# Scaling one token half only, and a second gate-up group with four seven-product pairs

## The chip, the cores and the metric

The kernel runs on one core of a Trainium2 chip. Time is device microseconds from launch to end; three runs of the kernel before gave 1823.62, 1824.14 and 1824.19 us, so the median is 1824.14 us. The engines are named as in the profile: PE is TensorE (matrix products), PEld its weight loads, DVE is VectorE, ACT is ScalarE, POOL is GpSimd and SP is SyncE, which here only issues DMAs.

## The reference

One encoder layer on 256 tokens of width 2048, in float32:

```python
ff = swiglu(rms_norm(x, pre_norm_ffn1), w_ffn1_gate_up, w_ffn1_down)   # 2048 -> 2 x 5632 -> 2048
x = x + 0.5 * rms_norm(ff, post_norm_ffn1)
h = rms_norm(x, pre_norm_mix)            # then HGRN2 heads and window attention on h @ w_mix_in
x = x + rms_norm(mixed, post_norm_mix)   # mixed = concat(y_h, y_a) @ w_mix_out
ff = swiglu(rms_norm(x, pre_norm_ffn2), w_ffn2_gate_up, w_ffn2_down)
x = x + 0.5 * rms_norm(ff, post_norm_ffn2)
```

`swiglu` is `silu(x @ gate) * (x @ up)` and then the down projection. The change is in the gate-up part of both feed-forward layers.

## The kernel before

**Exact products.** Every float32 operand is split into two parts, `h` (rounded) and `l` (the rest); a product is three matmuls, h by h, h by l and l by h. ScalarE writes `h` (line 176), VectorE subtracts to get `l` (line 177).

**Tiling of gate-up.** The 5632 gate and 5632 up columns are taken in 11 groups of 512 + 512 columns. Within a group the 2048 rows are taken in 8 pairs of two 128-row tiles. One pair of one group is one weight tile `raw` of 1 MB: four blocks of 128 x 512, b11 and b12 (gate and up of the first row tile), b21 and b22 (of the second). The tokens make a 2 x 2 block as well: two row tiles by two token halves of 128 tokens. A pair is thus a 2 x 2 by 2 x 2 block product. A plain pair takes 8 block products, that is 24 matmuls. A seven-product pair takes 7 (`products`, a Strassen-Winograd scheme), that is 21 matmuls, and needs sums of weight blocks and of token blocks. The four weight sums are made by an accumulating DMA that GpSimd issues (line 953, the up columns added onto b11 and b12 after b11 has been split) and two VectorE additions (lines 967 and 968); they also mean that the pair is split in three halves of 128 x 1024 and one first block of 128 x 512 instead of two halves. The token sums are made once for each pair by `sums_in` (lines 1069, 396, 399, 400 and one split), and serve all later groups.

**Which pairs.** `MIXED_IN = (2, 4, 5, 6)` lists the seven-product pairs. The first group is all plain. The second group (g = 1) has pairs 2 and 4 as sevens, every later group has all four. In the second group of the kernel before, the token sums of pairs 5 and 6 are made inside it (after pairs 4 and 5) for the third group.

**The scale of the norm.** The row norm gives one factor for each token, `rs2` (a column of two: token half 0 and 1). It is known only when the first group is under way. The first group therefore runs on unscaled tokens and applies `rs2` when it leaves PSUM (`units`, lines 1092 and 1097). For the token sums of a seven the two halves must have comparable scale, so the power of two of each factor (`two`) is spread over partitions (`spread`, a product with a matrix of ones, line 279) and multiplied into the token tiles in place (`even`, line 1062); the later groups apply what is left (`rest`).

**Order of the work.** From the second group on, each of TensorE, VectorE and ScalarE runs the order in which the code is written (`manual_schedule`). In the first group a scheduler places the instructions. Weight tiles come in through five buffers; `plan` sorts the loads by the time at which a pair is wanted, a seven-product pair some pairs ahead (`PREPARED`), and `prepare` splits its first block and issues the accumulating DMA. At the end of a group `boundary` adds the seven-product parts to the plain parts with eight VectorE additions (lines 1167 to 1177), between which TensorE does the last pair's products bank by bank.

Of the kernel before, what the change touches and what calls it, by code (L numbers as in the profile page):

```python
# [37 lines left out]
def hymba_layer_kernel(  # L38
# [25 lines left out]
    nc = tc.nc  # L64
# [18 lines left out]
    def pb():  # L83
        return psum.tile([P, 512], F32, tag="pb", name=nm("pb"))
# [16 lines left out]
    ones = const.tile([P, P], F32, tag="ones", name="ones")  # L101
# [35 lines left out]
    R = const.tile([P, T], F32, tag="R", name="R")  # L137
    scales = const.tile([P, 8], F32, tag="scales", name="scales")
    rs2, two, rest = (scales[:, 2 * i : 2 * i + 2] for i in range(3))

    def load(src, between=None, pool=rawp, **kw):
        raw = pool.tile([P, 2048], F32, tag="raw", name=nm("raw"), **kw)
# [122 lines left out]
    def power_and_rest():  # L265

        for part, a, b in ((two, 0x7F800000, 0), (rest, 0x007FFFFF, 0x3F800000)):
            nc.vector.tensor_scalar(
                part.bitcast(I32), rs2.bitcast(I32), a, b, ALU.bitwise_and, ALU.bitwise_or
            )  # L270

    def spread(factor=rs2):

        ps = pb()
        for m in range(2):
            nc.vector.tensor_scalar(
                R[:, m * P : (m + 1) * P], ident, factor[:, m : m + 1], None, ALU.mult
            )
        nc.tensor.matmul(ps[:, :T], ones, R, start=True, stop=True)
        nc.vector.tensor_copy(R, ps[:, :T])  # L280


    def xcol(xt, k, part=None):
# [599 lines left out]
    NG = DFF // 512  # L883
# [3 lines left out]
    MIXED_IN = (2, 4, 5, 6)  # L887
# [8 lines left out]
    class Gated(Blocks):  # L896
# [19 lines left out]

        def plan(self):

            self.here = {g: MIXED_IN if g > 1 else MIXED_IN[:2] for g in range(1, NG)}
            wanted = []  # L920
            for g in range(1, NG):
                for u in range(KT // 2):
                    before = PREPARED[u] if u in self.here[g] else u
                    wanted.append((g * KT // 2 + before, g, u))
            self.wanted = [at[1:] for at in sorted(wanted)]
            self.raws, self.firsts, self.split_of = {}, {}, {}
            self.lasting = []
# [96 lines left out]
    def ffn(gated, w_dn, post_gain, again, gain=None, lead=None, aside=None):  # L1024

        with ExitStack() as st:
# [31 lines left out]

            def even(u):

                x = gated.tiles[u].rearrange("p k i t -> p (k i) t")
                nc.vector.tensor_tensor(
                    x, x.bitcast(F32), R[:, None, :].to_broadcast([P, 4, T]), ALU.mult
                )

            def sums_in(u):
                x = gated.tiles[u].bitcast(F32)
                whole = room_for("z").rearrange("p (k t) -> p k t", k=2)
                nc.vector.tensor_tensor(whole, x[:, :, 0, :], x[:, :, 1, :], ALU.add)
                ws = sums_of(whole, room_for("s").rearrange("p (j t) -> p j t", j=4))  # L1070
                apart = u == MIXED_IN[1]
                w = (gated.room if apart else work).tile(
                    [P, 4, 2, P], F32R, tag="sp", name=nm("xs"), bufs=1 if apart else 3
                )
                split_act(w[:, :, 0, :], w[:, :, 1, :], ws)
                gated.sums[u] = w
# [63 lines left out]
            nc.scalar.activation(warm[:, 0:2], rs2, AF.Silu)  # L1140
            last = KT // 2 - 1
            for u in range(gated.pos, KT // 2):
                gated.work(u + 1)
                if u == 4:
                    power_and_rest()
                    spread(two)
                for done in {4: (0, 1, 2), 5: (3, 4), 6: (5, 6), 7: (7,)}.get(u, ()):
                    even(done)
                    if done in MIXED_IN[:2]:
                        sums_in(done)  # L1150
                if u == 5 and aside:
                    aside()
            gated.plan()
# [46 lines left out]
            def pair_ahead(g, u):  # L1200

                ahead = gated.splits(g, u + 1)
                next(ahead)
                if u + 1 == MIXED_IN[1]:
                    gated.prepare(g, MIXED_IN[3])
                next(ahead)
                for one in gated.take(g, u):
                    one()
                for _ in ahead:
                    pass  # L1210
                if g == 1 and u in (4, 5):
                    sums_in(MIXED_IN[u - 2])
                if u == 5 and 1 < g <= AWAY // 2 + 1:
                    put_away(2 * g - 4)
                    put_away(2 * g - 3)
# [163 lines left out]
    gated = Gated(w_ffn1_gate_up[0], two_banks())  # L1379
# [134 lines left out]
    with ExitStack() as s2:  # L1514
# [389 lines left out]
        g = gates(1)  # L1904
# [13 lines left out]
        gated = Gated(w_ffn2_gate_up[0], two_banks())  # L1918
# [80 lines left out]
```

## Time and profile before

| | us |
|---|---|
| median of three runs | 1824.14 |
| the profiled execution, its own time | 1824.91 |
| its span, first to last instruction | 1822.8 |
| PE busy | 1808.7 |
| DVE busy | 1607.0 |
| ACT busy | 1133.8 |
| POOL busy | 160.4 |

The times of the profile's views are counted from the span's start. A row of the timeline gives start, length, engine, source line, operation, tile written and tiles read, and in brackets the idle time ahead of it with what ended it. Lengths of neighbouring instructions of one engine overlap, since the next starts before the last one's write is through; where a cost is wanted, the step from one start to the next is used. In the first feed-forward layer the first group ends near 58 us and the second near 102 us; in the second layer the same work lies near 1168 and 1212 us.

### The profile page before, as it was taken

What the parts mean: (1) busy time and instruction counts of PE and PEld (TensorE: products, weight loads), DVE (VectorE), ACT (ScalarE), POOL (GpSimd) and SP (SyncE); (2) the same over time, 40 slices, a digit from 0 to 9 for tenths busy, and PEclk for the clock granted to TensorE, in tenths of its full rate; (3) what the DMA queues carried; (4) which work ended last, traced back from release to release, by engine and by line L of the source; (5) the groups of instructions that cost most, each with busy time, mean ns of one, the idle gap of its engine ahead of it and who ended that gap; (6) DMA issues with size and microseconds to landing.
All of it is one profiled execution on the core that took longest, in us unless ns stands there. A gap on an engine that the chain in (4) does not pass through costs nothing.

```text
span 1822.8 us, 23456 instructions
## 1 busy us (share of the span) xinstructions
PE 1808.7 (99%) x8426; PEld 1502.4 (82%) x8426; DVE 1607.0 (88%) x2059; ACT 1133.8 (62%) x1504; POOL 160.4 (9%) x153
## 2 busy tenths in 40 slices
PE   9999999999999999999999999999999999999998
PEld 6888888888888888888888888888888888888886
DVE  7999999999989989476787798999999999999987
ACT  7466666665665657476587556556666666566663
POOL 1011111111011100000000000001111111011110
PEclk9999999999999999999999999999999999999999
DMA  8789999998698995555554456789999998699894
GB/s 303 226 229 285 279 281 253 252 261 254 219 343 271 288 311 188 199 180 176 164 173 150 162 208 240 244 235 269 280 278 266 255 248 248 193 345 303 267 307 164
DMA packets 211508, 446.54 MB, mean 245 GB/s; under 512 B 11720, under 2 KB 46624, under 8 KB 210624
## 3 DMA queue, kind: packets, MB, share of 16 engines
q1 hardware_dynamic: 180032, 385.14, 60.4%
q0 software_dynamic: 31360, 59.91, 18.9%
q8 instruction: 66, 1.08, 0.2%
q14 instruction: 50, 0.41, 0.1%
HBM read 432.41 MB, written 12.60 MB: 244 GB/s over the span
## 4 chain that ended last, share of the span: by engine, by line
PE 95%; ACT 2%; DVE 2%; DMA 1%; issue 0%; SPq 0%; POOL 0%; DVEq 0%; ACTq 0%; POOLq 0%
PE pa L442 41%; PE pb L442 36%; PE pa L310 5%; PE pa L315 3%; PE pa L365 2%; PE pa L363 2%; PE pa L364 2%; DMA raw<-in_w_ffn_gate_up_dram 1%; DVE l L177 1%; PE pa L1117 1%; PE pb L1117 1%; PE pb L1720 0%; PE pb L1694 0%; PE pb L1798 0%; ACT h L176 0%
## 5 line engine op out<-in xcount | busy, mean ns | idle before, releaser
L176 ACT CAST h<-raw 128x1024 fp32r<-128x1024 f32 (+1 forms) x863 | 852.0, 1014 | 469.3 <-PE pb L442 151.0
L177 DVE TENSOR_TENSOR l<-raw,h 128x1024 fp32r<-128x1024 f32 (+1 forms) x863 | 984.5, 1171 | 133.8 <-ACT h L176 101.6
L442 PE MATMUL pa<-h,xt 128*128 128x512 f32 x1104 | 387.7, 392 | 0.1
L442 PE MATMUL pb<-h,xt 128*128 128x512 f32 x952 | 340.1, 392 | 0.4 <-DVE pb L1170 0.4
L442 PEld LDWEIGHTS pa<-h,xt 128*128 128x128 f32 x1104 | 207.2, 188 | 44.4 <-DVE xt L232 0.6
L442 PE MATMUL pa<-l,xt 128*128 128x512 f32 x552 | 215.4, 390 | 0.6 <-DVE l L177 0.5
L442 PEld LDWEIGHTS pb<-h,xt 128*128 128x128 f32 x952 | 178.6, 188 | 43.3 <-DVE pb L1177 3.7
L442 PE MATMUL pb<-l,xt 128*128 128x512 f32 x476 | 185.5, 390 | 0.0
L442 PE MATMUL pb<-h,ht 128*128 128x512 f32 x452 | 159.2, 389 | 0.0
L442 PE MATMUL pa<-h,ht 128*128 128x512 f32 x452 | 159.1, 389 | 0.0
L953 POOL DMA_DIRECT2D raw<-in_w_ffn_gate_up_dram x76 | 92.1, 1212 | 736.6 <-DVE l L177 639.1
L310 PE MATMUL pa<-xt,h 128*128 128x512 f32 x512 | 124.4, 392 | 0.2 <-ACT h L176 0.2
L442 PEld LDWEIGHTS pa<-l,xt 128*128 128x128 f32 x552 | 103.7, 188 | 21.4 <-DVE l L177 1.4
L310 PEld LDWEIGHTS pa<-xt,h 128*128 128x128 f32 x512 | 93.8, 188 | 18.6 <-ACT h L176 0.6
L442 PE MATMUL pa<-h,xs 128*128 128x512 f32 x304 | 108.8, 389 | 0.0
L442 PE MATMUL pb<-h,xs 128*128 128x512 f32 x304 | 105.9, 389 | 0.0
L442 PEld LDWEIGHTS pb<-l,xt 128*128 128x128 f32 x476 | 89.4, 188 | 17.0
L442 PEld LDWEIGHTS pb<-h,ht 128*128 128x128 f32 x452 | 84.8, 188 | 17.5
L442 PEld LDWEIGHTS pa<-h,ht 128*128 128x128 f32 x452 | 84.8, 188 | 17.5
L442 PE MATMUL pa<-l,ht 128*128 128x512 f32 x226 | 88.0, 389 | 0.0
L442 PE MATMUL pb<-l,ht 128*128 128x512 f32 x226 | 87.9, 389 | 0.0
L1255 POOL DMA_DIRECT2D raw<-in_w_ffn_down_dram x38 | 46.0, 1212 | 371.8 <-DVE la L177 317.6
(288 smaller groups left out, 2572.3 us busy)
## 6 DMA issues: line engine op xcount, KB each, us to landing
raw<-in_w_ffn_gate_up_dram SPq DMA_DIRECT2D x350, 512.0 KB, 6.0
raw<-in_w_ffn_down_dram SPq DMA_DIRECT2D x88, 1024.0 KB, 7.8
raw<-in_w_mix_in_dram SPq DMA_DIRECT2D x52, 1024.0 KB, 4.9
raw<-in_w_ffn_gate_up_dram POOLq DMA_DIRECT2D x76, 512.0 KB, 8.6
raw<-in_w_ffn_down_dram POOLq DMA_DIRECT2D x38, 512.0 KB, 10.0
raw<-in_w_mix_out_dram SPq DMA_DIRECT2D x16, 1024.0 KB, 5.2
ht<-away SPq DMA_DIRECT2D x24, 512.0 KB, 10.3
away<-ht SPq DMA_DIRECT2D x16, 512.0 KB, 7.3
```

Source lines behind the costliest of these rows:

```text
L176: nc.scalar.copy(hi, src)
L177: nc.vector.tensor_tensor(lo, src, hi.bitcast(F32), ALU.subtract)
L310: nc.tensor.matmul(slot[f], weights(hs, kk, f), xcol(xt, k), start=(k == 0), stop=(k == KT - 1))
L315: nc.tensor.matmul(slot[f][:, 0:T], weights(ls, kk, f), xcol(xt, kh * 8 + kk, 0), start=False, stop=False,)
L363: nc.tensor.matmul(dst, xh, h[:, o : o + n], start=(k == 0), stop=False)
L364: nc.tensor.matmul(dst, xh, l[:, o : o + n], start=False, stop=False)
L365: nc.tensor.matmul(dst, xl, h[:, o : o + n], start=False, stop=(k == KT - 1))
L442: nc.tensor.matmul(self.bank(at), lhs, rhs, start=(n == 1), stop=n in (ends, self.of[at]), skip_group_check=n > ends,)
L953: nc.gpsimd.dma_start(raw[:, 0:1024].rearrange("p (k c) -> p k c", k=2), self.source(u, g)[:, :, 1], accum_op=ALU.add,)
L1117: nc.tensor.transpose(bank[:, o : o + P], zs[m][:, k * P : (k + 1) * P], ident)
L1255: nc.gpsimd.dma_start(raws[i][:, 0:1024].rearrange("p (k c) -> p k c", k=2), Pairs.part(w_dn, u, r)[:, :, 512:1024], accum_op=ALU.add,)
```

## The change

Four things are edited, all in the gate-up part of both feed-forward layers.

The token tiles of half 0 are no longer scaled. Half 1 is multiplied by the ratio of the two powers of two (`ratio`), made by four small VectorE operations; `rest` is adapted so that the later groups' scales come out the same. `even` covers 4 x 128 elements on a partition instead of 1024, and `spread(ratio, 1)` makes one 128-column block instead of two.

`spread` is called inside pair 5 of the first group, after three of its eight block products, instead of after pair 4.

The second group takes all four pairs of `MIXED_IN` as sevens. The token sums of pair 5 are made at the end of the first group, those of pair 6 after pair 2 of the second group.

With that the load order of the second group becomes that of the later ones: pair 5 is loaded ahead of pair 3.

```diff
+        nc.vector.tensor_scalar(
+            ratio.bitcast(I32), two[:, 0:1].bitcast(I32),
+            0x7F800000, 0x7F800000, ALU.bitwise_and, ALU.bitwise_xor,
+        )
+        nc.vector.tensor_scalar(ratio, ratio, two[:, 1:2], 0.5, ALU.mult, ALU.mult)
+        nc.vector.tensor_scalar(rest[:, 1:2], rest[:, 1:2], two[:, 0:1], None, ALU.mult)
+        nc.vector.tensor_copy(rest[:, 0:1], rs2[:, 0:1])
...
-            self.here = {g: MIXED_IN if g > 1 else MIXED_IN[:2] for g in range(1, NG)}
+            self.here = {g: MIXED_IN for g in range(1, NG)}
+            for u in MIXED_IN:
+                self.sums.setdefault(u, None)
...
-                x = gated.tiles[u].rearrange("p k i t -> p (k i) t")
+                x = gated.tiles[u].rearrange("p k i t -> p (k i) t")[:, :, P:T]
                 nc.vector.tensor_tensor(
-                    x, x.bitcast(F32), R[:, None, :].to_broadcast([P, 4, T]), ALU.mult
+                    x, x.bitcast(F32), R[:, None, 0:P].to_broadcast([P, 4, P]), ALU.mult
                 )
...
-                gated.work(u + 1)
+                if u == 5:
+                    gated.work(u + 1, lambda: spread(ratio, 1))
+                else:
+                    gated.work(u + 1)
                 if u == 4:
                     power_and_rest()
-                    spread(two)
-                for done in {4: (0, 1, 2), 5: (3, 4), 6: (5, 6), 7: (7,)}.get(u, ()):
+                for done in {5: (0, 1, 2, 3, 4), 6: (5, 6), 7: (7,)}.get(u, ()):
                     even(done)
                     if done in MIXED_IN[:2]:
                         sums_in(done)
+                if u == 7:
+                    sums_in(MIXED_IN[2])
...
-                if g == 1 and u in (4, 5):
-                    sums_in(MIXED_IN[u - 2])
+                if g == 1 and u == 2:
+                    sums_in(MIXED_IN[3])
```

On VectorE, in the second group, the stretch from pair 5 to pair 6 stood like this (l is the subtracted part of a half, raw a weight tile, z and s the working tiles of the token sums, xs the split sums):

```order
L177 TENSOR_TENSOR l_846<-raw_630,h_845 128x1024
L177 TENSOR_TENSOR l_850<-raw_630,h_849 128x1024
L1069 TENSOR_TENSOR z_876<-xt_124 128x512
L396 TENSOR_TENSOR s_878<-z_876 128x2x128
L399 TENSOR_TENSOR s_878<-s_878,z_876 128x128
L400 TENSOR_TENSOR s_878<-z_876,s_878 128x128
L177 TENSOR_TENSOR xs_882<-s_878,xs_882 128x4x128
L177 TENSOR_TENSOR l_886<-raw_636,h_885 128x1024
L177 TENSOR_TENSOR l_890<-raw_636,h_889 128x1024
```

And with the change:

```order
L178 TENSOR_TENSOR l_877<-raw_651,h_876 128x1024
L981 TENSOR_TENSOR raw_651<-raw_651 128x512
L982 TENSOR_TENSOR raw_651<-raw_651 128x512
L178 TENSOR_TENSOR l_883<-raw_651,h_882 128x1024
L178 TENSOR_TENSOR l_908<-raw_651,h_907 128x1024
L178 TENSOR_TENSOR l_914<-raw_648,h_913 128x1024
L981 TENSOR_TENSOR raw_648<-raw_648 128x512
L982 TENSOR_TENSOR raw_648<-raw_648 128x512
L178 TENSOR_TENSOR l_920<-raw_648,h_919 128x1024
L178 TENSOR_TENSOR l_945<-raw_648,h_944 128x1024
```

Pairs 5 and 6 have three halves and two block additions each, and the chains of token sums that stood between them are gone from there; pair 5's is in the first group now, pair 6's further up.

On VectorE, at the end of the first group of the first layer, the scaling of the token tiles (R is the spread factor, xt the token tiles) began before the change as:

```order
L276 TENSOR_SCALAR R<-ident,scales 128x128 x2
L177 TENSOR_TENSOR l_562<-raw_554,h_561 128x1024
L280 COPY R<-pb_469 128x256
L1062 TENSOR_TENSOR xt_123<-xt_123,R 128x1024 x4
L1069 TENSOR_TENSOR z_477<-xt_123 128x512
```

And with the change:

```order
L288 TENSOR_SCALAR R<-ident,scales 128x128
L178 TENSOR_TENSOR l_565<-raw_557,h_564 128x1024
L178 TENSOR_TENSOR l_598<-raw_594,h_597 128x1024
L292 COPY R<-pb_493 128x128
L1076 TENSOR_TENSOR xt_123<-xt_123,R 128x4x128 x4
L1083 TENSOR_TENSOR z_515<-xt_123 128x512
```

One more weight half is split ahead of the copy that waits for the spreading product, and each scaling is half as wide.

On GpSimd the accumulating DMAs that follow the table's write-out stood like this (raw_627 is pair 2 and raw_633 pair 4 of the second group, the rest is the third group):

```order
L1473 DMA row<-bias_rows 8x512
L953 DMA raw_627<-in_w_ffn_gate_up_dram 128x2x512
L953 DMA raw_633<-in_w_ffn_gate_up_dram 128x2x512
L953 DMA raw_639<-in_w_ffn_gate_up_dram 128x2x512
L953 DMA raw_630<-in_w_ffn_gate_up_dram 128x2x512
```

And with the change, where raw_651 is pair 5 and raw_648 pair 6 of the second group and raw_642 the first of the third:

```order
L1491 DMA row<-bias_rows 8x512
L967 DMA raw_639<-in_w_ffn_gate_up_dram 128x2x512
L967 DMA raw_645<-in_w_ffn_gate_up_dram 128x2x512
L967 DMA raw_651<-in_w_ffn_gate_up_dram 128x2x512
L967 DMA raw_648<-in_w_ffn_gate_up_dram 128x2x512
L967 DMA raw_642<-in_w_ffn_gate_up_dram 128x2x512
```

Two accumulating DMAs are added to each layer, between the second and the third that stood there.

More of the change, by code (lines that the diff above doesn't have):

```diff
@@ L139, in hymba_layer_kernel @@
     rs2, two, rest = (scales[:, 2 * i : 2 * i + 2] for i in range(3))
+    ratio = scales[:, 6:7]
     def load(src, between=None, pool=rawp, **kw):
@@ L270, in power_and_rest, with spread @@
             )
-    def spread(factor=rs2):
+        nc.vector.tensor_scalar(
+            ratio.bitcast(I32),
+            two[:, 0:1].bitcast(I32),
+            0x7F800000,
+            0x7F800000,
+            ALU.bitwise_and,
+            ALU.bitwise_xor,
+        )
+        nc.vector.tensor_scalar(ratio, ratio, two[:, 1:2], 0.5, ALU.mult, ALU.mult)
+        nc.vector.tensor_scalar(rest[:, 1:2], rest[:, 1:2], two[:, 0:1], None, ALU.mult)
+        nc.vector.tensor_copy(rest[:, 0:1], rs2[:, 0:1])
+    def spread(factor=rs2, n=2):
         ps = pb()
-        for m in range(2):
+        for m in range(n):
             nc.vector.tensor_scalar(
@@ L278, in spread @@
             )
-        nc.tensor.matmul(ps[:, :T], ones, R, start=True, stop=True)
-        nc.vector.tensor_copy(R, ps[:, :T])
+        nc.tensor.matmul(ps[:, : n * P], ones, R[:, : n * P], start=True, stop=True)
+        nc.vector.tensor_copy(R[:, : n * P], ps[:, : n * P])
     def xcol(xt, k, part=None):
```

## The prediction

> **What bounds the kernel now.** I read the page first: its time by engine, and the chain that ended last.
>
> ```profile
> span 1822.8 us, 23456 instructions
> PE 1808.7 (99%) x8426; PEld 1502.4 (82%) x8426; DVE 1607.0 (88%) x2059; ACT 1133.8 (62%) x1504; POOL 160.4 (9%) x153
> PE 95%; ACT 2%; DVE 2%; DMA 1%; issue 0%; SPq 0%; POOL 0%; DVEq 0%; ACTq 0%; POOLq 0%
> ```
>
> TensorE carries the chain, so a product taken out of it looks like time saved. VectorE, at 88%, is close behind. The shares are means over stages, so next come the waits of TensorE and two stretches of the first layer: 71 to 113 us is roughly the second group, 113 to 155 us the third.
>
> ```profile
> PE pb L442 <- DVE pb L1170: 0.4, 2, 0.2
> ...
> 71.00:113.00 42.00, 41.80 (x188) 34.18 (x187) 38.68 (x52) 23.26 (x29) 3.62 (x3) 1.00 0.76 223
> 113.00:155.00 42.00, 42.00 (x191) 34.57 (x190) 40.01 (x48) 26.19 (x30) 4.82 (x4) 1.00 0.95 282
> ```
>
> The columns of the last two are the stretch, its length, then busy time of PE, PEld, DVE, ACT and POOL, the granted clock, the DMA share and GB/s. The third group has four sevens, and VectorE is busy 40.0 of its 42 us; the second has two sevens and two chains of token sums, and VectorE is busy 38.7. The one wait of TensorE in feed-forward work that is counted here twice, once in each layer, is at the end of exactly the group that is changed. TensorE's timeline there shows its size:
>
> ```profile
> 96.64 0.39 PE L442 MATMUL pa<-h,xt 128*128 128x512 f32 x1
> 97.23 0.50 PE L442 MATMUL pb<-h,xt 128*128 128x512 f32 x1 [0.20 <-DVE pb L1170]
> ```
>
> From one product to the next it is 0.59 us instead of 0.23 (below), so 0.36 us are lost, though the row counts 0.20. TensorE is waiting for a boundary addition of VectorE. So at the end of the second group VectorE already sets the time, and what the change does to VectorE before that point counts, not only what it takes from TensorE.
>
> **TensorE's side.** The chain of waits from 63 to 76 us shows a plain pair (24 products) and a seven (21):
>
> ```profile
> 64.37 1.38 PE pa L442 x6
> 65.75 1.36 PE pb L442 x6
> 67.11 1.36 PE pa L442 x6
> 68.47 1.36 PE pb L442 x6
> 69.83 2.72 PE pa L442 x12
> 72.55 2.04 PE pb L442 x9
> ```
>
> One product costs 1.36 / 6 = 0.227 us. Two more sevens take away six, 1.36 us in each layer. The spreading product:
>
> ```profile
> 39.66 0.39 PE L442 MATMUL pb<-h,xt 128*128 128x512 f32 x1
> 39.89 0.59 PE L279 MATMUL pb<-R,ones 128*128 128x256 f32 x2
> 40.13 0.58 PE L442 MATMUL pa<-h,xt 128*128 128x512 f32 x1
> 40.55 0.40 PE L442 MATMUL pa<-l,xt 128*128 128x512 f32 x1
> ```
>
> From 39.89 to 40.55 lie the spread and one product: 0.66 - 0.23 = 0.43 us for 256 columns. Half the columns save 0.21. TensorE has 1.57 us less to do in each layer, 3.1 us in both, 0.17%. That is the most this change can bring through products alone.
>
> **VectorE's side, in one layer.** The rows that price it:
>
> ```profile
> 38.69 0.24 DVE L268 TENSOR_SCALAR scales<-scales 128x2 int32<-128x2 int32 x2
> 38.90 0.48 DVE L276 TENSOR_SCALAR R<-ident,scales 128x128 f32<-128x128 f32 x2
> ...
> 40.52 0.42 DVE L280 COPY R<-pb 128x256 f32<-128x256 f32 x1
> 40.98 4.63 DVE L1062 TENSOR_TENSOR xt<-xt,R 128x1024 fp32r<-128x1024 f32 x4
> 45.53 0.68 DVE L1069 TENSOR_TENSOR z<-xt 128x512 f32<-128x512 f32 x1
> 46.13 1.22 DVE L1062 TENSOR_TENSOR xt<-xt,R 128x1024 fp32r<-128x1024 f32 x1
> ...
> 66.26 0.69 DVE L967 TENSOR_TENSOR raw<-raw 128x512 f32<-128x512 f32 x1
> 66.99 0.69 DVE L968 TENSOR_TENSOR raw<-raw 128x512 f32<-128x512 f32 x1
> 67.60 1.22 DVE L177 TENSOR_TENSOR l<-raw,h 128x1024 fp32r<-128x1024 f32 x1
> 68.73 0.68 DVE L177 TENSOR_TENSOR ht<-z,ht 128x512 fp32r<-128x512 f32 x1
> ...
> 102.86 0.68 DVE L177 TENSOR_TENSOR l<-raw,h 128x512 fp32r<-128x512 f32 x1
> 103.46 0.74 DVE L1097 SCALAR_TENSOR_TENSOR s<-pb,scales,s 128x512 f32<-128x512 f32 x1
> ```
>
> From start to start:
> - Scaling: four of 1024 elements take 45.53 - 40.98 = 4.55, so 1.14 each; one of 512 takes 46.13 - 45.53 = 0.60 (line 1069, the same operation and element type). The strided half tile is not in the trace; between 0.60 and 1.14 I take 0.60, since its element count is that of the 512 row. Eight scalings save 8 x 0.54 = 4.3 us.
> - The spread: one of two 0.2 us scalings of the identity goes and half of a 0.42 us copy: 0.3 us saved. The four new small operations cost 0.1 each, 0.4.
> - A seven in place of a plain pair adds the first block (103.46 - 102.86 = 0.60), the two block additions (0.73 and 0.61) and a third half (68.73 - 67.60 = 1.13): 3.1 us, and 0.1 of waiting between dependent rows. Two of them: 6.4 us.
> - The number of token sums is the same, four; they only move.
>
> Sum: 6.4 + 0.4 - 4.3 - 0.3 = +2.2 us of work before the boundary. Can idle time take it up? From the end of the small operations to the first boundary addition VectorE has these gaps:
>
> ```profile
> 58.54 1.23 DVE L177 TENSOR_TENSOR l<-raw,h 128x1024 fp32r<-128x1024 f32 x1 [0.54 <-ACT h L176]
> ...
> 81.20 1.23 DVE L177 TENSOR_TENSOR l<-raw,h 128x1024 fp32r<-128x1024 f32 x1 [0.64 <-ACT h L176]
> ...
> 84.83 0.69 DVE L177 TENSOR_TENSOR xs<-s,xs 128x512 fp32r<-128x512 f32 x1 [0.69 <-ACT xs L176]
> 85.77 2.36 DVE L177 TENSOR_TENSOR l<-raw,h 128x1024 fp32r<-128x1024 f32 x2 [0.26 <-ACT h L176]
> ...
> 94.36 0.69 DVE L1167 TENSOR_TENSOR pa<-pa,z 128x512 f32<-128x512 f32 x1
> ```
>
> The pair of 0.69 and 0.26 is one chain of token sums: VectorE makes the sums, waits while ScalarE rounds them, then waits once more. It occurs twice in the second group (again for pair 6). Pair 5's goes to the first group's end, where the scheduler puts other rows between: 0.95 saved. The 0.64 at 81.20 is a wait from being ahead, and late work fills it. The 0.54 at 58.54 is another matter:
>
> ```profile
> ACT h L176 <- DMA raw<-in_w_ffn_gate_up_dram: 8.9, 3, 5.6
> ```
>
> ScalarE waits there (56 to 101 us) for the second group's first weights, which come no earlier after the change; VectorE arrives with 4.3 us less scaling done behind it, so this gap rather grows. I put that at 0.4, within the 5.6 us of the longest such wait, and 0.2 for the two new pairs' dependent rows. VectorE is then late at the first boundary addition by 2.2 - 0.95 - 0.64 + 0.4 + 0.2 = 1.2 us. TensorE comes earlier and waits for it. The end of the group moves with VectorE: +1.2 us. Bounds from the rows: all hidden, -1.57; nothing absorbed and the two additions of 0.4 and 0.2 in full, 2.2 + 0.6 = +2.8.
>
> **What else moves.** GpSimd issues two more accumulating DMAs in each layer.
>
> ```profile
> raw<-in_w_ffn_gate_up_dram POOLq DMA_DIRECT2D x76, 512.0 KB, 8.6
> ```
>
> They are 0.5 MB each and land in 8.6 us (median). GpSimd is busy 9% and nothing else of the second group stands in its queue. The DMA share there is 0.76; the third group carries as many accumulates and put-away tiles too at 0.95 without a wait of TensorE, so I cost the traffic at nothing; if that cover is gone, pair 6's accumulate lands late and VectorE, which has no spare time, pays each microsecond. On SP pair 5's load passes pair 3's; the third group has that order already, at no wait. ScalarE, 23 of 42 us busy, gets one cast of a first block and one of a half more for each new seven and has room. The later spread delays the scaling by three block products (9 x 0.23 = 2.0 us); the first scaled tile is needed only when the second group begins, two pairs on, so nothing is late.
>
> After the boundary VectorE has 2 us to spare in each later group (40.0 of 42), so the lateness is not carried on. The second layer has the same wait at the same place and the same work: +1.2 again. In sum 2.4 us: 1824.91 + 2.4 = 1827.3 for an execution like the profiled one, which was 0.77 above the median; against the median 1824.14, 1826.5.
>
> **Rivals.**
> 1. *VectorE hides it.* If VectorE has 1.2 + 1.57 = 2.8 us more slack in the stretch than the row of 81.20 shows, the whole 3.1 us are gained: 1821.0. For it speaks that the third group holds four sevens with no counted wait; against it, that the second group has a chain of sums more and that its boundary is where TensorE waits now. Were the boundary losses (0.36 each) to go as well, it would be 1820.3, just past 0.2% faster.
> 2. *VectorE is the bound throughout, so its work adds in full* (ends slower). Nothing of 2.2 + 0.6 is absorbed, in either layer: 2 x 2.8 = +5.6, 1829.7. It decides from 1.8 us a layer. For it speaks the 1.2 us estimate, which rests on 1.6 us of gaps closing; a late accumulate for pair 6 has the same effect. Against it, VectorE's idle time is real in the rows above. The Trainium skill (Perfetto Trace Analysis, Identifying the Most-Contended Engine) says to rank engines by occupancy, but TensorE by its weight-load share, not its matmul share. By that rule VectorE's 88% stands above the weight loads' 82% and VectorE is what bounds the kernel, as in this rival. The trace agrees at the second group's boundary and disagrees elsewhere, where TensorE's waits are next to nothing.
> 3. *The two cancel.* The gap at 58.54 closes as well and the lateness is 0.5 or less: within 1 us of 1824.1. I count it with the forecast, since only its size differs.
>
> **How the numbers follow.** About 0.2%, 3.65 us, is what a measurement of this kernel can tell from no change. The forecast (+0 to +3.6, with 3) has 0.53, and the time is 1826.5. Rival 2 has 0.35, rival 1 has 0.12, of which 0.04 lies beyond 0.2%. So faster 0.04, same 0.61, slower 0.35. The range leaves out most of rival 1 and the upper end of rival 2: 1822.0 to 1830.0.
>
> **What the profile after would show.** Right: in the second group TensorE waits for VectorE, by l of pairs 4 to 6 and by the first boundary addition, 2 to 3 us in each layer, while it has six products fewer there; the scaling rows step by 0.60; VectorE has next to no gap from 60 us to the boundary; the third group shows nothing new. Wrong: TensorE without new waits (rival 1), or boundary additions more than 1.8 us later than before (rival 2), above all behind a wait for an accumulate.

## The result, and the profile after

The changed kernel took 1827.50 us (median of 19 runs, 1825.63 to 1828.99), the kernel before beside it 1823.95 us (19 runs, 1823.34 to 1824.96): +3.55 us, a ratio of 1.0018 with a 95% interval of 1.0011 to 1.0025 (+2.0 to +4.6 us). The forecast was +2.4 and a time of 1826.5 in a range of 1822.0 to 1830.0. It is a loss just under the 0.2% that the prediction took as its bound.

The page after, its time by engine and the chain that ended last:

```profile
span 1825.9 us, 23473 instructions
PE 1806.8 (99%) x8414; PEld 1499.0 (82%) x8414; DVE 1610.8 (88%) x2081; ACT 1139.6 (62%) x1512; POOL 165.3 (9%) x157
PE 89%; DVE 5%; ACT 3%; issue 2%; DMA 1%; SPq 0%; POOL 0%; DVEq 0%; ACTq 0%; POOLq 0%
```

TensorE has twelve products fewer, and the share of VectorE in the chain rose from 2% to 5%. The waits of TensorE, the three groups that belong to the gate-up code (total us, times, longest):

```profile
PE pa L454 <- DVE pa L1185: 2.5, 2, 1.3
PE pa L454 <- DVE l L178: 2.4, 5, 0.6
...
PE pb L454 <- DVE pb L1188: 0.9, 2, 0.5
```

Before, the boundary additions had one group of 0.4 us, and `l` one wait of 0.5 us at the start of the kernel, which is there still (0.61 us) among the five; three of the five lie in the second groups (0.61 and 0.62 in the first layer, 0.40 in the second). All three groups have VectorE as the releaser, and those of the boundary additions occur twice, once a layer. In the first layer's second group, TensorE's timeline:

```profile
82.08 0.50 PE L454 MATMUL pa<-l,xs 128*128 128x512 f32 x1 [0.61 <-DVE l L178]
...
91.94 0.50 PE L454 MATMUL pa<-l,xs 128*128 128x512 f32 x1 [0.62 <-DVE l L178]
...
96.71 0.50 PE L454 MATMUL pa<-h,xt 128*128 128x512 f32 x1 [1.25 <-DVE pa L1185]
...
98.83 0.50 PE L454 MATMUL pb<-h,xt 128*128 128x512 f32 x1 [0.47 <-DVE pb L1188]
```

The products that wait for `l` belong to pair 4 and to pair 6: token sums (xs) with the second half that is split, the one behind the two block additions. The other two are the last pair's products behind the first and the fourth boundary addition. The two stretches that the prediction showed, now:

```profile
71.00:113.00 42.00, 39.04 (x172) 30.64 (x171) 40.25 (x49) 24.39 (x30) 4.82 (x4) 1.00 0.84 236
113.00:155.00 42.00, 42.00 (x191) 34.65 (x190) 39.99 (x48) 26.47 (x31) 4.86 (x4) 1.00 0.94 279
```

In the first one TensorE's busy time fell from 41.80 to 39.04 us and VectorE's rose from 38.68 to 40.25; the second one is as before.

Where the time came in is read best from a mark in each group. TensorE transposes the finished group's tiles right behind the first pair of the next group, so from one such transposition to the next is one group. The first transposition after the first and after the second group, in each layer, before:

```profile
63.34 0.27 PE L1117 MATMUL pa<-ident,z 128*128 128x128 f32 x1
...
107.02 0.27 PE L1117 MATMUL pa<-ident,z 128*128 128x128 f32 x1
...
1173.36 0.27 PE L1117 MATMUL pa<-ident,z 128*128 128x128 f32 x1
...
1217.06 0.27 PE L1117 MATMUL pa<-ident,z 128*128 128x128 f32 x1
```

and after:

```profile
62.51 0.27 PE L1131 MATMUL pa<-ident,z 128*128 128x128 f32 x1
...
108.63 0.27 PE L1131 MATMUL pa<-ident,z 128*128 128x128 f32 x1
...
1174.60 0.27 PE L1131 MATMUL pa<-ident,z 128*128 128x128 f32 x1
...
1219.50 0.27 PE L1131 MATMUL pa<-ident,z 128*128 128x128 f32 x1
```

The step of the second group was 43.68 us in the first layer and 43.70 in the second. It is 46.12 and 44.90 after: +2.44 and +1.20. The same step of the third group is 41.83 and 41.78 before, 41.80 and 41.80 after, and the later groups don't give anything back.

The third group also says what the second could take with no loss. It has four sevens and takes 41.80, so two sevens would be 41.80 + 2 x 0.68 = 43.16 and three 42.48. The loss in the second group was therefore 0.52 us in each layer before (43.68 - 43.16). It is 4.32 in the first layer and 3.10 in the second after. TensorE's 1.36 us were saved, and 2.6 to 3.8 us of new waiting came for them (4.32 and 3.10 less 0.52).

### The profile page after: what moved, and what is told of

The parts are those of the page before. It is cut to its first block, busy times and chain, and to the rows that moved or that the text cites. A ratio compares the mean times of both kernels' runs of the same rounds, so it can differ in the third digit from the quotient of the medians.

```text
span 1825.9 us, 23473 instructions
## 1 busy us (share of the span) xinstructions
PE 1806.8 (99%) x8414; PEld 1499.0 (82%) x8414; DVE 1610.8 (88%) x2081; ACT 1139.6 (62%) x1512; POOL 165.3 (9%) x157
## 4 chain that ended last, share of the span: by engine, by line
PE 89%; DVE 5%; ACT 3%; issue 2%; DMA 1%; SPq 0%; POOL 0%; DVEq 0%; ACTq 0%; POOLq 0%
PE pa L454 38%; PE pb L454 33%; PE pa L322 5%; DVE l L178 3%; PE pa L327 3%; PE pa L377 2%; PE pa L376 2%; PE pa L375 2%; ACT h L177 1%; DMA raw<-in_w_ffn_down_dram 1%; PE pa L1131 1%; PE pb L1131 1%; PE pb L1738 0%; PE pb L1712 0%; PE pb L1816 0%
## 5 line engine op out<-in xcount | busy, mean ns | idle before, releaser
L454 PE MATMUL pa<-h,xt 128*128 128x512 f32 x1088 | 382.0, 392 | 2.7 <-DVE pa L1185 2.5
L454 PE MATMUL pb<-h,xt 128*128 128x512 f32 x928 | 332.4, 391 | 0.9 <-DVE pb L1188 0.9
L454 PEld LDWEIGHTS pb<-h,xt 128*128 128x128 f32 x928 | 174.1, 188 | 42.5 <-DVE pb L1195 3.4
L454 PE MATMUL pb<-l,xt 128*128 128x512 f32 x464 | 180.9, 390 | 0.0
L967 POOL DMA_DIRECT2D raw<-in_w_ffn_gate_up_dram x80 | 97.0, 1212 | 735.7 <-DVE l L178 681.4
L454 PE MATMUL pa<-h,xs 128*128 128x512 f32 x320 | 114.8, 389 | 0.0
L454 PE MATMUL pb<-h,xs 128*128 128x512 f32 x320 | 111.6, 389 | 0.0
```

Of the source, the lines that this page charges most:

```text
L454: nc.tensor.matmul(self.bank(at), lhs, rhs, start=(n == 1), stop=n in (ends, self.of[at]), skip_group_check=n > ends,)
L967: nc.gpsimd.dma_start(raw[:, 0:1024].rearrange("p (k c) -> p k c", k=2), self.source(u, g)[:, :, 1], accum_op=ALU.add,)
```

## Experiments

Each kernel was timed beside the kernel before on the same chip; the differences below are against the median of before in the same call. The table has the step of the second group in each layer, read from the two transpositions as above, and the loss against 41.80 us plus 0.68 for each pair that is left plain.

| kernel | us | before | difference | ratio, 95% | step 1, loss | step 2, loss |
|---|---|---|---|---|---|---|
| after | 1827.50 | 1823.95 | +3.55 | 1.0011 to 1.0025 | 46.12, 4.32 | 44.90, 3.10 |
| scale_only | 1824.05 | 1824.15 | -0.10 | 0.9990 to 1.0007 | 43.68, 0.52 | 43.70, 0.54 |
| sevens_only | 1835.33 | 1824.15 | +11.18 | 1.0048 to 1.0074 | 48.01, 6.21 | 48.20, 6.40 |
| three | 1822.59 | 1824.15 | -1.56 | 0.9984 to 1.0002 | 43.23, 0.75 | 42.75, 0.27 |
| table_apart | 1825.91 | 1824.15 | +1.76 | 1.0001 to 1.0019 | 44.15, 2.35 | 44.93, 3.13 |
| more_vec | 1830.18 | 1824.54 | +5.64 | 1.0017 to 1.0041 | 47.90, 6.10 | 45.82, 4.02 |
| three_table | 1822.85 | 1824.54 | -1.69 | 0.9981 to 0.9998 | 42.74, 0.26 | 42.75, 0.27 |
| three_six | 1826.30 | 1824.54 | +1.76 | 1.0001 to 1.0018 | 46.33, 3.85 | 43.90, 1.42 |
| three_sums | 1821.74 | 1824.45 | -2.71 | 0.9976 to 0.9995 | 42.40, -0.08 | 42.42, -0.06 |

The interval of one row is 2.6 to 4.7 us wide. Differences of 1 or 2 us between two versions therefore don't follow from the times alone; they rest on the steps, each read from the one execution that was profiled. That of three_six was the slowest of its eleven (1828.41), 2.1 us above the median; those of three and three_sums were 1.3 and 1.6 above theirs.

My theory was that VectorE sets the end of the second group once it has four sevens. The rivals were that transfers do it (first weights, accumulates), or the plain length of the boundary's chain of additions.

### The two halves of the change apart

**scale_only**: the halved scaling and the later spread, with two sevens.

```diff
-            self.here = {g: MIXED_IN for g in range(1, NG)}
-            for u in MIXED_IN:
-                self.sums.setdefault(u, None)
+            self.here = {g: MIXED_IN if g > 1 else MIXED_IN[:2] for g in range(1, NG)}
...
-                if u == 7:
-                    sums_in(MIXED_IN[2])
...
-                if g == 1 and u == 2:
-                    sums_in(MIXED_IN[3])
+                if g == 1 and u in (4, 5):
+                    sums_in(MIXED_IN[u - 2])
```

> The halved scaling and the spread alone; the second group keeps two sevens and makes the token sums for pairs 5 and 6 where the kernel before does. Theory A, VectorE already sets the time at the second group's boundary in the kernel before (the step of the prediction): VectorE comes there with 4.3 + 0.3 - 0.4 = 4.2 us less work, so the 0.36 us that TensorE loses after the row of 97.23 goes, in both layers, and the spread saves 0.21 twice: 1823.95 - 0.7 - 0.4 = 1822.8. Theory B, the 0.36 us is the length of the chain of dependent boundary additions, whatever VectorE did before: the gap stays, only the spread counts, 1823.5. In both the first boundary addition of the first layer need not move, since VectorE is held at the second group's first weights.

Measured: -0.10 us, not told apart from no change. The steps of the second group are those of before to the hundredth, and TensorE's timeline shows the boundary's gap unchanged:

```profile
95.69 0.39 PE L454 MATMUL pa<-h,xt 128*128 128x512 f32 x1
96.28 0.50 PE L454 MATMUL pb<-h,xt 128*128 128x512 f32 x1 [0.20 <-DVE pb L1184]
```

0.59 from start to start, as before. So theory A of this run falls: 4.2 us less work of VectorE ahead of the second group does nothing for its end. What is left of the gain is the narrower spread: from the copy of the norm's second factor to the second transposition it is 0.19 and 0.16 us shorter than before, where 0.21 was priced. VectorE has its time back as waiting:

```profile
54.93 1.23 DVE L178 TENSOR_TENSOR l<-raw,h 128x1024 fp32r<-128x1024 f32 x1 [1.94 <-ACT h L177]
...
80.24 1.22 DVE L178 TENSOR_TENSOR l<-raw,h 128x1024 fp32r<-128x1024 f32 x1 [1.49 <-ACT h L177]
```

It waits for ScalarE's `h` at 54.93 and again at 80.24; whatever was saved before such a wait is lost in it, and what it still has to do from the last one to the boundary is the same. What that tail holds, three_sums shows below.

**sevens_only**: the two more sevens and the earlier token sums, with the scaling and the spread of before.

```diff
-                x = gated.tiles[u].rearrange("p k i t -> p (k i) t")[:, :, P:T]
+                x = gated.tiles[u].rearrange("p k i t -> p (k i) t")
                 nc.vector.tensor_tensor(
-                    x, x.bitcast(F32), R[:, None, 0:P].to_broadcast([P, 4, P]), ALU.mult
+                    x, x.bitcast(F32), R[:, None, :].to_broadcast([P, 4, T]), ALU.mult
                 )
...
-                if u == 5:
-                    gated.work(u + 1, lambda: spread(ratio, 1))
-                else:
-                    gated.work(u + 1)
+                gated.work(u + 1)
                 if u == 4:
                     power_and_rest()
+                    spread(two)
-                for done in {5: (0, 1, 2, 3, 4), 6: (5, 6), 7: (7,)}.get(u, ()):
+                for done in {4: (0, 1, 2), 5: (3, 4), 6: (5, 6), 7: (7,)}.get(u, ()):
```

> The two more sevens and the early token sums alone, with the scaling at full width (eight of 1.14 us) and the spread of two factors. Theory A, VectorE sets the time of the second group: against the kernel after it has 4.3 + 0.3 - 0.4 = 4.2 us more work in each layer, of which the first layer can hide the 1.25 us by which the gap at the second group's first weights had grown; with the wider spread (2 x 0.21): 1827.5 + 8.4 - 1.25 + 0.4 = 1835.1. Theory B, the loss of the kernel after is set by transfers (first weights, accumulates) and not by VectorE's work: little more than 1827.5 + 0.4 = 1827.9. Theory C, TensorE alone counts: 1823.95 - 2 x 1.36 = 1821.2.

Measured: 1835.33, where theory A said 1835.1 and the others 1827.9 and 1821.2. TensorE's waits, the groups of the gate-up code (the first with the one at the kernel's start):

```profile
PE pa L442 <- DVE l L177: 3.5, 5, 1.0
PE pa L442 <- DVE pa L1171: 2.5, 2, 1.3
PE pa L1119 <- DVE s L1099: 2.1, 2, 1.2
...
PE pa L1119 <- DVE z L1099: 0.8, 1, 0.8
```

Two groups are new beside those of the kernel after, 2.9 us in all: the transpositions of the first group (line 1119) now wait for VectorE's gating products as well. VectorE's lateness reaches back into the first group's end. From the copy of the norm's second factor to the second transposition the way is 3.0 us longer than in the kernel after in the first layer and 4.5 in the second, where theory A gives 4.2 + 0.2, less 1.25 in the first. So the halved scaling with the later, narrower spread was worth 11.18 - 3.55 = 7.6 us once four sevens stood behind it, and next to nothing with two.

### Is it VectorE's work, and all of it?

**more_vec**: four operations more for VectorE in the second group. The code says two places; pair 1's turn is handled by another function (`first_pairs`), so only the four after pair 3 are there, in each layer.

```diff
                 if g == 1 and u == 2:
                     sums_in(MIXED_IN[3])
+                if g == 1 and u in (1, 3):
+                    for _ in range(4):
+                        nc.vector.tensor_scalar(
+                            R[:, 0:P], R[:, 0:P], 1.0, None, ALU.mult
+                        )
```

> The kernel after with eight more operations of VectorE in the second group of each layer (128 x 128, the factors R times 1.0, four after pair 1 and four after pair 3; each waits for the one before it). At the 0.27 us of a row of this size plus 0.06 of a dependent row, about 0.3 each: 2.4 us in each layer. Theory A, VectorE sets the end of the second group: all of it shows at the first boundary addition, 1827.5 + 2 x 2.4 = 1832.3. Theory B, the loss is set by transfers or by ScalarE, and VectorE has time to spare: 1827.5.

VectorE's timeline shows what was added in each layer:

```profile
83.17 1.01 DVE L1233 TENSOR_SCALAR R<-R 128x128 f32<-128x128 f32 x4
...
1195.63 1.00 DVE L1233 TENSOR_SCALAR R<-R 128x128 f32<-128x128 f32 x4
```

That is 1.0 us a layer (0.92 to the start of the next row, at 84.09 in the first layer), not 2.4, so theory A says about +2 against the kernel after and not +4.8. Measured: 5.64 - 3.55 = +2.1 us. In the second layer the step grew by 0.92, all that was added. In the first it grew by 1.78; there the first group's end came 0.8 us earlier in this run (61.73). From the copy of the norm's second factor to the second transposition the first layer is 1.39 longer than in the kernel after, 0.92 of it the added work and 0.40 longer waits of VectorE (3.51 in place of 3.11).

**three**: the kernel after with one seven fewer in the second group (pair 6 plain).

```diff
-            self.here = {g: MIXED_IN for g in range(1, NG)}
-            for u in MIXED_IN:
+            self.here = {g: MIXED_IN if g > 1 else MIXED_IN[:3] for g in range(1, NG)}
+            for u in MIXED_IN[:3]:
                 self.sums.setdefault(u, None)
...
-                if g == 1 and u == 2:
+                if g == 1 and u == 5:
                     sums_in(MIXED_IN[3])
```

> The kernel after with three sevens in the second group in place of four (pairs 2, 4 and 5; pair 6 plain, its token sums at the end of pair 5's turn). Per layer against the kernel before: TensorE 3 products (0.68) and 0.21 less, VectorE 3.2 + 0.4 - 4.3 - 0.3 = 1.0 us less. Theory A, the kernel after loses because VectorE is late at the boundary by 2.19 us in the first layer and 1.01 in the second, above what TensorE gains: one seven less takes 3.2 us from VectorE, so it is no longer late and TensorE's saving is had in full: 1823.95 - 2 x 0.89 = 1822.2, without waits of TensorE by l in the second group. Rival, the transfers of the early token sums and the accumulates set the loss: about 1825.5 or more, with TensorE still waiting behind l of pair 5.

Measured: 1822.59, 1.56 us below before (expected 1822.2; the interval of the ratio just includes 1). TensorE has three products more than after in each layer, and the kernel is 5 us faster than after. TensorE's timeline shows no wait for `l` in the second group any more. In the first layer one wait is left, at the place of the boundary's old one (0.20 before):

```profile
95.30 0.50 PE L454 MATMUL pb<-h,xt 128*128 128x512 f32 x1 [0.36 <-DVE pb L1188]
```

So between three and four sevens the bound of this group passes from TensorE to VectorE. In the second layer the third group loses a little as well, in this run and in three_table (42.03 and 42.07 us).

### The first weights of the first layer

In the first layer the loss was 1.2 us larger than in the second. VectorE's and ScalarE's timelines of the kernel after, where the second group's first tile is split:

```profile
53.62 1.05 ACT L177 CAST h<-raw 128x1024 fp32r<-128x1024 f32 x1 [1.24 <-DMA raw<-in_w_ffn_gate_up_dram]
56.64 1.05 ACT L177 CAST h<-raw 128x1024 fp32r<-128x1024 f32 x1 [1.98 <-PE pb L454]
```

```profile
54.70 1.23 DVE L178 TENSOR_TENSOR l<-raw,h 128x1024 fp32r<-128x1024 f32 x1 [0.52 <-ACT h L177]
...
57.72 1.23 DVE L178 TENSOR_TENSOR l<-raw,h 128x1024 fp32r<-128x1024 f32 x1 [1.27 <-ACT h L177]
```

The gap of VectorE that was 0.54 before is 0.52 + 1.27 = 1.79 now, 1.25 more. Only the first layer makes a table of attention biases here (`spread_bias`), in one of the three raw buffers. GpSimd writes it out, and the loads that follow on SP's queue wait for that. GpSimd's row, and the DMA view from 44 to 62 us (40 slices of 0.45 us, and the issue):

```profile
47.07 0.55 POOL L1491 DMA_DIRECT2D row<-bias_rows  x1 [9.20 <-DVE s L411]
```

```profile
GB/s 401 123 0 0 0 0 0 0 36 37 0 0 0 0 0 0 146 269 364 401 373 369 351 73 96 164 273 282 391 360 346 273 250 250 241 228 273 250 323 337
...
row<-bias_rows POOLq DMA_DIRECT2D x1, 16.0 KB, 2.7
```

Issued at 47.07, landed near 49.8; the next load is issued at 49.9, and but for the table nothing moves from 45 to 51 us.

**table_apart**: the kernel after with the table in a tile of the hidden pool that isn't in use yet.

```diff
-    def spread_bias():
+    def spread_bias(early):
...
-        rows = rawp.tile([P, 2048], F32, tag="raw", name="bias_rows")
+        rows = early.tile([P, 2, 2, T], F32R, tag="ht", name="bias_rows").bitcast(F32)
+        rows = rows.rearrange("p k i t -> p (k i t)")
...
-        vec = rows[0:HEADS, 2 * REL_W : 3 * REL_W]
+        vec = ng
```

> The kernel after, with the rows of the bias table (first layer only) in a tile of the hidden pool instead of one of the three raw buffers, so that the second group's first weights need not wait until the table is written out. Theory A, in the first layer VectorE loses 1.25 us more than before in the gaps of 0.52 and 1.27 ahead of 54.70 and 57.72 because those weights are issued only after the table's write-out (issued at 47.07, 2.7 us to landing): the gaps go, the first boundary addition comes about 1.2 us earlier than 95.96, 1827.5 - 1.2 = 1826.3, and the second layer is as it was. Rival B, VectorE only waits elsewhere instead (for ScalarE's rounding of the token sums, or for TensorE to free a buffer of h): 1827.5 as before. Rival C, with another order of the three buffers a product of the first group waits: 1828 and more.

Measured: 1825.91 (+1.76 where the kernel after has +3.55): 1.8 us, a little over the 1.2 of theory A. The step of the first layer fell from 46.12 to 44.15, that of the second stayed (44.90, 44.93). From the copy of the norm's second factor (38.12) to the first boundary addition (94.39) it is 56.27 us in the first layer, where the kernel after took 58.05. VectorE runs through the place without a gap until it meets a chain of token sums:

```profile
50.92 1.21 DVE L178 TENSOR_TENSOR l<-raw,h 128x1024 fp32r<-128x1024 f32 x1
...
53.07 1.21 DVE L178 TENSOR_TENSOR l<-raw,h 128x1024 fp32r<-128x1024 f32 x1
...
57.27 0.69 DVE L178 TENSOR_TENSOR xs<-s,xs 128x512 fp32r<-128x512 f32 x1 [0.69 <-ACT xs L177]
```

So the table's buffer is shown to be the cause of the wait. Whether the cast at 56.64 waited for the landing or, as its row says, for a buffer of `h` that TensorE held, was not tried apart.

**three_table**: the same with three sevens, both edits together.

> Three sevens in the second group and the bias table's rows outside the raw buffers. The table alone took 1.6 us from the kernel after. Theory A, an earlier landing of the first weights helps only where VectorE sets the time; with three sevens TensorE does, so nothing changes: 1822.6. Rival, the landing is a cost of its own for this layer: 1822.6 - 1.6 = 1821.0.

Measured: -1.69 against -1.56 for three: by the times no gain is seen, though their intervals alone would not exclude the rival's 1.6 us. The way from the copy of the norm's second factor to the second transposition decides: in the first layer it is 67.37 us in three and 67.53 here (theory A). The step is 0.49 shorter only because the first group ends later. In these runs the late landing cost time with four sevens, where VectorE is the bound, and none with three.

### Sum of the work, or its place?

**three_six**: three sevens again, of pairs 2, 4 and 6.

```diff
-            self.here = {g: MIXED_IN if g > 1 else MIXED_IN[:3] for g in range(1, NG)}
-            for u in MIXED_IN[:3]:
+            self.here = {g: MIXED_IN if g > 1 else (2, 4, 6) for g in range(1, NG)}
+            for u in (2, 4, 6):
...
-                    sums_in(MIXED_IN[2])
+                    sums_in(MIXED_IN[3])
...
-                    sums_in(MIXED_IN[3])
+                    sums_in(MIXED_IN[2])
```

> Three sevens in the second group, of pairs 2, 4 and 6 in place of 2, 4 and 5; pair 5 is plain, and its token sums are made at the end of its turn, pair 6's ahead of the group. The same products and the same VectorE work before the boundary as with pairs 2, 4 and 5 (1822.59). Theory A, the sum of VectorE's work up to the boundary decides: 1822.6 again. Rival, the place decides: the seven's rows of pair 6 stand between the chain of pair 5's token sums (0.69 + 0.26 us of gaps) and the boundary additions, with nothing left to catch up in, so TensorE waits by l of pair 6 and at the boundary by about 1 us a layer: 1824.6.

Measured: +1.76, 3.3 us worse than three with the same work: the place decides, and by more than the rival's 2 us. The second layer shows the rival alone: its step is 1.15 us longer than in three (43.90 and 42.75), and TensorE waits at the boundary. In the first layer VectorE meets besides a wait that the kernel after does not have. The rows of its timeline are GpSimd's accumulate for pair 6, VectorE's block addition behind it, and TensorE at the boundary:

```profile
78.36 1.20 POOL L967 DMA_DIRECT2D raw<-in_w_ffn_gate_up_dram  x1 [15.40 <-DVE l L178]
```

```profile
86.12 0.69 DVE L981 TENSOR_TENSOR raw<-raw 128x512 f32<-128x512 f32 x1 [1.74 <-DMA raw<-in_w_ffn_gate_up_dram]
...
92.36 0.69 DVE L178 TENSOR_TENSOR xs<-s,xs 128x512 fp32r<-128x512 f32 x1 [0.69 <-ACT xs L177]
```

```profile
96.94 0.50 PE L454 MATMUL pa<-h,xt 128*128 128x512 f32 x1 [2.04 <-DVE pa L1185]
```

The accumulate issued at 78.36 lands 7.6 us later, VectorE stands for 1.74, then makes pair 5's sums with their gaps of 0.69 and 0.26, and TensorE waits 2.04. With pairs 2, 4 and 5 the last accumulate of the group is long in by then (issued at 64.90 at the latest, with at most 8.2 us to landing). This is the late accumulate that the prediction named under its second rival: real, though not in this change. As this is the slowest execution of the eleven, how much of it the others have is not known.

**three_sums**: three_table with pair 6's token sums two pairs earlier in the second group.

```diff
-                if g == 1 and u == 5:
+                if g == 1 and u == 3:
                     sums_in(MIXED_IN[3])
```

> Three sevens, the table apart, and pair 6's token sums at the end of pair 3's turn in the second group instead of pair 5's. Question: what makes the 0.36 us that TensorE loses at the second group's boundary before the change, which stayed when VectorE got 4.2 us less to do earlier. Theory A, the tail decides: the chain of token sums with its gaps of 0.69 and 0.26 stands between VectorE's last catching up with TensorE and the boundary; two pairs earlier, the gaps are taken up and the loss at the boundary goes, in both layers: 0.3 to 0.7 less than with the table apart alone, about 1822.3 beside a kernel before of 1824.5. Theory B, the four dependent additions of the boundary are that long by themselves: the loss stays, 1822.85.

Measured: 1821.74, 2.71 us below before, with an interval that no longer includes 1, and 1.0 better than three_table: theory A. The step of the second group is 42.40 and 42.42, where 42.48 was worked out for three sevens with no loss; three_table has 42.74 and 42.75, and another 0.22 more in the third group of the second layer. VectorE now comes to the boundary ahead of TensorE:

```profile
93.13 0.70 DVE L1185 TENSOR_TENSOR pa<-pa,z 128x512 f32<-128x512 f32 x1 [1.34 <-PE pa L454]
```

So the four boundary additions are not too long in themselves. Before the change the same chain of token sums, with nearly 1 us in which VectorE stands still, lies in the last pair ahead of the boundary; that it is what made TensorE wait there is argued from these runs with three sevens and was not tried with two. The chain moves as a whole, so its pauses and its work (0.69 + 0.26 us, and some 2.5 us of rows) are not told apart either. This version is 0.9986 of before, 0.9976 to 0.9995.

## Why the prediction came out as it did

**The forecast, +2.4, and its sign: right.** +3.55 was measured, with +2.4 inside the interval. By the traces it is +2.2 in the first layer and +1.0 in the second, where +1.2 and +1.2 were forecast. This is the way from the copy of the norm's second factor, which comes ahead of all that was changed, to the first boundary addition. Before (the first layer's addition, at 94.36, stands in the prediction):

```profile
38.50 0.15 DVE L263 COPY scales<-r 128x1 f32<-128x1 f32 x1 [0.67 <-POOL r L186]
...
1144.45 0.15 DVE L263 COPY scales<-r 128x1 f32<-128x1 f32 x1 [0.73 <-POOL r L186]
...
1204.40 0.69 DVE L1167 TENSOR_TENSOR pa<-pa,z 128x512 f32<-128x512 f32 x1
```

and after:

```profile
37.91 0.15 DVE L264 COPY scales<-r 128x1 f32<-128x1 f32 x1 [0.67 <-POOL r L187]
...
95.96 0.69 DVE L1185 TENSOR_TENSOR pa<-pa,z 128x512 f32<-128x512 f32 x1
...
1145.87 0.15 DVE L264 COPY scales<-r 128x1 f32<-128x1 f32 x1 [0.73 <-POOL r L187]
...
1206.83 0.69 DVE L1185 TENSOR_TENSOR pa<-pa,z 128x512 f32<-128x512 f32 x1
```

58.05 - 55.86 = 2.19 and 60.96 - 59.95 = 1.01. The rest of the 3.55 lies within the spread of the runs. TensorE's new waits in the second group are 2.95 us in the first layer and 2.13 in the second; the prediction's sign of being right was 2 to 3.

**The work of VectorE, +2.2: right; the 0.2 for dependent rows: counted twice.** The halved scaling steps by 0.60 as taken from the other row, four of them here:

```profile
42.03 2.50 DVE L1076 TENSOR_TENSOR xt<-xt,R 128x512 fp32r<-128x512 f32 x4
44.45 0.68 DVE L1083 TENSOR_TENSOR z<-xt 128x512 f32<-128x512 f32 x1
```

(44.45 - 42.03) / 4 = 0.605. The rest follows from the gaps. Besides the two ahead of 54.70 and 57.72 VectorE has these in the kernel after, on the first layer's way from the copy to the boundary:

```profile
40.53 1.23 DVE L178 TENSOR_TENSOR l<-raw,h 128x1024 fp32r<-128x1024 f32 x1 [0.37 <-ACT h L177]
...
76.66 0.69 DVE L178 TENSOR_TENSOR xs<-s,xs 128x512 fp32r<-128x512 f32 x1 [0.69 <-ACT xs L177]
77.61 1.23 DVE L178 TENSOR_TENSOR l<-raw,h 128x1024 fp32r<-128x1024 f32 x1 [0.26 <-ACT h L177]
```

All five are 1.79 + 0.37 + 0.95 = 3.11, where the prediction's rows had 0.54 + 0.64 + 0.95 + 0.95 = 3.08. So work in itself is 2.19 - 0.03 = 2.16 us more. In the second layer the gaps are 4.38 in place of 5.58, and work is 1.01 + 1.20 = 2.21 more. Both are the forecast's 2.2. The further 0.2 didn't show: the price of a seven, 3.1 and 0.1, already held the wait between dependent rows, in its steps of 0.73 and in the 0.1.

**The mis-sized term: "this gap rather grows. I put that at 0.4".** It grew by 1.25 in the first layer. The prediction knew that the first weights come no earlier and that 4.3 us of scaling lay behind them. It then took 0.4 where the row bounded it only by 5.6. A second gap, the 0.37 at 40.53, it put at nothing: there VectorE waits for `h` of the weight half that is now split ahead of the spread's copy. Together with the 0.2 that didn't show, 0.85 + 0.37 - 0.24 is the 1.0 by which the first layer came out above 1.2. The prediction also took the gap for one of both layers, but its growth hangs on the bias table, which only the first layer makes: with the table elsewhere the first layer's step fell by 1.97. In the second layer, which has no table, the sum of the prediction held (+1.0 for +1.2), in part by luck. The waits ahead of the second group grew by 0.77 there, where 0.4 was forecast, and the wait that late work filled, at 1191.23, was 1.02 long, where 0.64 was taken from the first layer.

**"The 0.64 at 81.20 is a wait from being ahead, and late work fills it": right**, and so is pair 5's 0.95. After 60 us VectorE has just one chain's 0.69 and 0.26 left in the first layer.

**"So at the end of the second group VectorE already sets the time": right of the place, wrong of the reason.** The prediction read it as too much work. With 4.2 us less work ahead of the group the loss of 0.36 stayed (scale_only); with the chain of sums two pairs earlier it went (three_sums). By the runs with three sevens it was the place of a chain with idle time in it, close to the end. The term of this is small, since the wait was not what the change altered most, but the reading "what the change does to VectorE before that point counts" needs its condition: it counts only if VectorE doesn't stand waiting in between.

**Rival 1, VectorE hides it: excluded.** The loss of the second group went from 0.5 to 3.1 and 4.3.

**Rival 2, nothing absorbed, +2.8 a layer: between.** The first layer, at 2.2, passed the 1.8 from which the rival was to decide, but not by the rival's reason: 1.59 of idle time was taken up there as forecast, and new waits of 1.62 came in its place. The second stayed at 1.0. By the rule of the Trainium skill cited there (Perfetto Trace Analysis, Identifying the Most-Contended Engine), taken by the weight loads alone (the page puts the matmul FLOP utilization beside them), VectorE's 88% against the weight loads' 82% make it the bound of the kernel. The runs agree for one group out of eleven, where 0.92 us of added VectorE work cost 0.92 in the second layer. They disagree for the later groups, whose step is 41.80 us and where TensorE is busy without a pause (42.00 of 42 us in the stretch of the third). A share over the whole kernel could not tell the two apart. The same page (Optimization Strategy) says that the most contended engine can change between regimes of one kernel; the traces agree, with a change of bound at one group's border.

**What was costed at nothing.** The accumulates, the load order on SP and ScalarE: after 60 us VectorE waited in the second group for no accumulate, and for ScalarE only in the one chain of token sums, so this held. That it need not is shown by three_six, where 1.74 us came from one. The later spread also held: scale_only, which has it, costs nothing.

## What to carry to other kernels

When two engines are within a few per cent of each other, price a trade for the stage it is made in: read that stage's step from mark to mark beside the step of a stage that has no loss, and trade only up to the point at which the other engine takes over (three sevens here, not four). Of the engine that becomes late, follow the idle time and not only the work: savings ahead of a wait are lost in it, and a chain with pauses in it should stand far from the point where the other engine waits (in these runs two pairs were enough). A wait that one layer has and the other hasn't can hang on something unrelated that is done there, here a table in a weight buffer.

## What the runs showed of the hardware beside

In three_six, the accumulating DMA of 0.5 MB for pair 6 was issued 6.0 us before VectorE was ready for it in the first layer (78.36, and VectorE idle from 84.38), and VectorE waited 1.74 us. In the second layer it was issued 7.3 us ahead (1189.56, used at 1196.85) and landed after 6.9; VectorE did not wait for it, though ScalarE did (0.98). With 5.6 to 8.8 us from issue to landing for the accumulates between 60 and 100 us of the kernel after, a place some 6 us ahead is too near. The runs of the kernel after are spread over 3.4 us where those of before in the same call are spread over 1.6; sevens_only, the slowest, is spread over 0.9 (5 runs). I have no cause for that.
